# Hybrid decoder layer: token sums spawned before the last two gate tiles, and the first pair's weights spawned between the two halves of the memory values

## The chip, the cores and the metric

The kernel runs on one core of one Trainium2 chip. The metric is device microseconds of one execution; three runs of the kernel before took 1953.37, 1948.39 and 1949.68 us, median 1949.68 us. Profile rows name the engines PE (matrix), PEld (weight loads of PE), DVE (vector), ACT (scalar), POOL (GpSimd) and SP (which issues the DMAs).

## The reference, cut to what matters

One decoder layer over 1024 tokens of 1024 channels. The normalised input goes through one wide projection; three branches (a gated delta rule, differential attention, attention into a 256-token memory) are gated and merged.

```python
h = rms_norm(x, pre_w)
[gdn_qkv, gdn_a, gdn_b, gdn_z, dq, dk, dv, dz, mq, mz, gate_logits] = [h @ w_in[:, lo:hi] for lo, hi in bounds]
...                                        # branch 1: gated delta rule over 8 heads
oa = rms_norm(oa, gdn_norm_w) * jax.nn.silu(gdn_z.reshape(b, s, GDN_HEADS, GDN_DV))
...
m = rms_norm(mem, mem_norm_w)              # the memory: keys and values
mk, mv = jnp.split(m @ w_mem_kv, 2, axis=-1)
...
return x + rms_norm(y @ w_out, post_w)
```

All is float32. A product is made on PE from two-part numbers: each operand is split into a rounded high part and a low part, and three matmuls (high*high, high*low, low*high) are added up.

## The kernel before, in words

The work lies in stages, one behind the other on PE: (1) delta-rule projections, scans and eight **gate tiles** z0 to z7 of the first branch; (2) the **memory keys**, eight tiles k0 to k7; (3) the **memory values**, two halves of eight row blocks; (4) a long stage in which all other input projections are made in pairs by **Strassen's method** (seven products per pair instead of eight), beside attention; (5) the three branch outputs and the output projection. The change lies at the seam of stages 1 to 4, some 540 to 630 us into the run.

**A gate tile** is `zmul` (L265 to 273): a product `gemm` (L206, matmuls L219, L220 and L224), silu on ACT (L269), then a multiplication on DVE (L272) and a store (L273).

**A weight load** is `wsplit` (L161 to 170): 256 KB from DRAM into a tile `wr` (three buffers), a rounded high part `wh` made by ACT (L167), and the low part `wl` = `wr` - `wh` by DVE (L169), two buffers each. A `wr` buffer is free again when its `wl` is made. The matmul L224 (in the keys L776, in the values L788) needs `wl`. A gate tile takes two such loads, a key tile two, each half of the values eight.

**The memory** is normalised by `mem_norm` (L738): squares on ACT (L750), a power on POOL (L158) between two DVE steps (L157, L753), transposes on PE (L759), then a split into `mh` and `ml` (ACT L763, DVE L764). `mem_keys` (L768) and `mem_values` (L780) follow; a finished key tile is split out of PSUM by ACT and DVE (L734, L735).

**The token sums** are `combine_tokens` (L804): Strassen's method needs eight sums and differences of quarters of the tokens, in four rounds j = 0 to 3. Each round makes eight 128x512 sums on DVE (L810 to L819) and splits four of them (ACT L734, DVE L735). The results lie in tiles `o` and `q` for the whole of stage 4.

**The pairs' weights**: `upper` (L843) forms a sum of weight quarters in a `wr` buffer (L852) and its high part on ACT (L854); `lower` (L856) makes the low part on DVE (L858). `strassen` (L877) makes them three products ahead of the one on PE.

**What sets the order.** Side work is written as generators: `spawn` puts one in a list, and each `tick` (called while a product is written down, or by `until`) advances every one by a step. A scheduling layer below then makes of this one list per engine, and it does move instructions against the order of the text; an engine runs its list strictly in order, and so does the DMA queue of SP. In the profile, the list of the kernel before has the first round of token sums (L810) right behind the gate multiplication of z5, ahead of the memory's normalisation (L753): the tiles `hi`, `lo` and `x` lie in memory that the first branch frees at that point.

Of the kernel before, what the change touches and what calls it, by code (L numbers as in the profile page):

```python
# [10 lines left out]
F32R = mybir.dt.float32r  # L11
# [5 lines left out]
P = 128  # L17
S = 1024
D = 1024
KT = D // P  # L20
# [31 lines left out]
def hybrid_layer_kernel(  # L52
# [125 lines left out]
    def spawn(gen):  # L178
        threads.append(gen)
# [14 lines left out]
    def until(cond):  # L194
        while not cond():
            tick()
# [68 lines left out]
    def zmul(n, zcol, tile_):  # L265

        pz = gemm(w_in, zcol + n * P, hh, hl)
        sz = tile_()
        A.activation(sz, pz, AF.Silu)  # L269
        until(lambda: n in os)  # L270
        o = os.pop(n)
        V.tensor_tensor(o, o, sz, op=ALU.mult)  # L272
        nc.sync.dma_start(oscr[0][n], o)  # L273
# [441 lines left out]
    def xtile(shape=(P, S), dt=F32):  # L715
        return xp.tile(list(shape), dt, name=nm("x"), tag="x", bufs=9)
# [87 lines left out]
    def combine_tokens():  # L804

        for j in range(4):
            (b1, (u0, u1)), (b2h, b2l) = lower[j], upper[j]
            b11, b12, b21, b22 = (hit((P, 512), F32) for _ in range(4))
            f32 = lambda t: t.bitcast(F32)
            V.tensor_tensor(b11, f32(b1[:, 0]), f32(b1[:, 1]), op=ADD)  # L810
            V.tensor_tensor(b12, f32(u0[:, :]), f32(u1[:, :]), op=ADD)
            for b, sl in ((b21, slice(0, 512)), (b22, slice(512, 1024))):
                V.tensor_tensor(b, f32(b2h[:, sl]), f32(b2l[:, sl]), op=ADD)
            yield
            t2 = lot((P, 512), F32)
            V.tensor_tensor(b11, b12, b11, op=SUB)
            V.tensor_tensor(t2, b22, b11, op=SUB)
            V.tensor_tensor(b12, b22, b12, op=SUB)
            V.tensor_tensor(b21, b21, t2, op=SUB)  # L819
            yield  # L820
            for p, src, new in ((5, b11, ot), (6, t2, ot), (7, b12, qt), (4, b21, qt)):
                t = new((P, 2, 512), F32R)
                split(t[:, 0], t[:, 1], src)
                comb[p].append((t[:, 0], t[:, 1]))
                yield
# [52 lines left out]
    def strassen(pairs):  # L878
        seq = [(q, p) for q in pairs for p in ORDER]

        def upper(n):
            if n < len(seq):
                seq[n][0].upper(seq[n][1])

        def lower(n):
            if n < len(seq):
                seq[n][0].lower(seq[n][1])

        pairs[0].load(True)
        pairs[0].load(False)  # L890
        upper(0)
        lower(0)
        upper(1)
        lower(1)
        upper(2)
        for n, (q, p) in enumerate(seq):
            if p in (1, 6) and n + 7 < len(seq):
                seq[n + 7][0].load(p == 1)
            lower(n + 2)
            upper(n + 3)  # L900
            q.multiply(p)
# [103 lines left out]
        return Pair((c, c + P), through(False, gts[bi][n:n + 2], ("gate", bi, n // 2)))  # L1005

    spawn(mem_norm())
    zmul(6, C_Z, xtile)
    zmul(7, C_Z, xtile)
    until(lambda: "mem" in ready)  # L1010
    spawn(combine_tokens())
    for n in range(2):
        mk = [xtile((P, 4, MEM), F32R) for _ in range(2)]
        for i in range(4):
            mem_keys(4 * n + i, mk)
        for h in range(2):
            for u in range(2):
                nc.sync.dma_start(mkd[2 * n + h][:, :, u], mk[u][:, 2 * h:2 * h + 2].bitcast(F32))
    mv = [[xtile((P, D), F32R) for _ in range(2)] for _ in range(2)]
    for f in range(2):  # L1020
        mem_values(f, mv)
        for h in range(2 * f, 2 * f + 2):
            for t in range(2):
                for u in range(2):
                    nc.sync.dma_start(mvd[h][:, t, u], mv[t][u][:, h * MEM:(h + 1) * MEM].bitcast(F32))
# [253 lines left out]
        ready.add("attention")  # L1279
        yield from make0  # L1280

    pairs = []
    for h in range(H):
        pairs.append(key_query(h))
        pairs.append(silu_z(1, C_DZ, h - 1) if h % 2 else values_pair(h))
    for h in range(4):
        pairs.append(mem_query(h))
        pairs.append(silu_z(2, C_MZ, 2 * h))
    pairs += [gates(b, n) for b in range(3) for n in range(0, KT, 2)]

    spawn(attention())
    pace[0] = 2
    new_banks()
    strassen(pairs)
    new_banks()
    ready.add("pairs")
    pace[0] = 6
# [68 lines left out]
    pw = xtile()  # L1366
    nc.sync.dma_start(pw, post_w.to_broadcast([P, D]))

    def products(po, t, ks, f):
        ts_ = slice(t * P, (t + 1) * P)  # L1370
        for k in ks:
            for lt, rt in ((yh, wh), (yh, wl), (yl, wh)):
                T.matmul(po[f], lhsT=lt[k][:, ts_], rhs=rt[k][f],  # L1373
                         start=(k == 0 and lt is yh and rt is wh), stop=(k == 7 and lt is yl))
# [4 lines left out]
    pos = {t: columns() for t in range(2)}  # L1379
    for t in range(2):  # L1380
        for f in range(2):
            products(pos[t], t, range(4), f)
    for t in range(NT):

        ts_ = slice(t * P, (t + 1) * P)
# [2 lines left out]
        nc.sync.dma_start(xr, x[ts_, :])  # L1388
        ss = small([P, 2], "oss", 4)
        for f, sl in enumerate(half):  # L1390
            products(po, t, range(4 if t < 2 else 0, KT), f)
            A.activation(res[:, sl], po[f], AF.Square, scale=1.0 / 32, accum_out=ss[:, f:f + 1])
        rs = small([P, 1], "rs", 4)
        V.tensor_scalar(rs, ss[:, 0:1], ss[:, 1:2], EPS, op0=ADD, op1=ADD)
# [29 lines left out]
```

## Time and profile before

| | us |
|---|---|
| median of three runs | 1949.68 |
| the profiled execution, its own time | 1953.46 |
| span of its trace | 1951.3 |
| PE busy | 1880.8 |
| DVE busy | 1261.0 |
| ACT busy | 930.9 |

Line numbers are those of the kernel before. In a timeline a row gives the start, the duration, engine, line, operation, output <- inputs, shape and count, and in brackets the idle time just before it with what ended it. Rows of the same kind that follow each other are merged (x12). The trace's busy PE includes matmuls that overlap, so a step from one start to the next is a better price than a duration. Granted clock 1.00 is 2.4 GHz, 0.50 is 1.2 GHz; a window between the two holds some of each.

### The profile page before, as it was taken

How to read it: one execution, taken by the hardware profiler on the slowest of the kernel's cores; microseconds unless marked ns; L12 is line 12 of the kernel's file. 1: busy time of each engine (PE TensorE's matmuls, PEld its weight loads, DVE VectorE, ACT ScalarE, POOL GpSimd, SP SyncE). 2: the span in 40 equal slices, each digit the busy share in tenths (PEclk: the TensorE clock that was granted, in tenths of full speed). 3: DMA queues.
4: the chain of work that ended last, by engine and by line, in shares of the span. 5: the costliest groups of instructions: out<-in, count | busy, mean ns of one | idle time of the engine just before them, and what ended most of it. 6: DMA issues, size and time to landing. Idle time of an engine off the chain costs nothing.

```text
span 1951.3 us, 28521 instructions
## 1 busy us (share of the span) xinstructions
PE 1880.8 (96%) x10231; PEld 1564.6 (80%) x10231; DVE 1261.0 (65%) x2578; ACT 930.9 (48%) x2057; POOL 140.5 (7%) x115
## 2 busy tenths in 40 slices
PE   7999999999997999999999999999999999999998
PEld 5778888788885787878888878888878777888886
DVE  5786778764395687878887777766666553434432
ACT  5543563545354565666655555655444451212211
POOL 1230131302101000000000000000000000000011
PEclk9998999999999999999999999999999999999999
DMA  3323131422265656555645345443466468565522
GB/s 127 97 84 101 37 92 47 111 61 60 65 201 158 195 157 195 153 178 168 187 152 177 115 150 167 149 152 109 162 232 205 146 232 264 195 204 175 159 87 87
DMA packets 292609, 282.44 MB, mean 145 GB/s; under 512 B 40066, under 2 KB 224756, under 8 KB 292468
## 3 DMA queue, kind: packets, MB, share of 16 engines
q1 hardware_dynamic: 292468, 280.63, 45.9%
q8 instruction: 80, 1.31, 0.3%
q14 instruction: 61, 0.50, 0.1%
HBM read 189.27 MB, written 91.29 MB: 144 GB/s over the span
## 4 chain that ended last, share of the span: by engine, by line
PE 75%; DVE 9%; DMA 6%; issue 5%; ACT 3%; POOL 2%; SPq 1%; DVEq 0%; POOLq 0%; ACTq 0%
PE bank L868 28%; PE acc L219 9%; PE acc L224 9%; PE acc L220 9%; PE sd L1156 3%; PE sd L1144 2%; PE sd L1111 2%; PE sd L1110 1%; DMA x<-mqd 1%; PE sd L1373 1%; PE sd L474 1%; PE sd L1215 1%; DMA wr<-in_w_mem_kv_dram 1%; DVE wl L169 1%; DVE u L975 1%
## 5 line engine op out<-in xcount | busy, mean ns | idle before, releaser
L868 PE MATMUL bank<-h,hi 128*128 128x512 f32 x864 | 282.0, 399 | 2.8 <-DVE x L735 2.8
L219 PE MATMUL acc<-h,wh 128*128 128x512 f32 x548 | 225.2, 412 | 4.2 <-DVE y L437 2.5
L167 ACT CAST wh<-wr 128x512 fp32r<-128x512 f32 x144 | 89.4, 621 | 286.4 <-PE acc L220 249.8
L220 PE MATMUL acc<-h,wh 128*128 128x512 f32 x548 | 215.8, 394 | 0.2 <-DVE h L735 0.2
L868 PE MATMUL bank<-o,hi 128*128 128x512 f32 x576 | 189.6, 402 | 2.4 <-ACT u L873 2.4
L868 PE MATMUL bank<-q,hi 128*128 128x512 f32 x576 | 187.9, 400 | 2.5 <-DVE u L923 2.3
L868 PEld LDWEIGHTS bank<-h,hi 128*128 128x128 f32 x864 | 160.8, 190 | 33.5 <-issue 3.5
L224 PE MATMUL acc<-h,wl 128*128 128x512 f32 x548 | 181.7, 393 | 0.6 <-DVE wl L169 0.6
L169 DVE TENSOR_TENSOR wl<-wr,wh 128x512 fp32r<-128x512 f32 x144 | 104.1, 725 | 105.3 <-ACT wh L167 99.0
L868 PE MATMUL bank<-h,lo 128*128 128x512 f32 x432 | 171.8, 398 | 0.0
L854 ACT CAST hi<-wr 128x512 fp32r<-128x512 f32 x144 | 89.2, 620 | 121.6 <-PE bank L868 120.4
L858 DVE TENSOR_TENSOR lo<-wr,hi 128x512 fp32r<-128x512 f32 x144 | 99.8, 693 | 51.5 <-PE bank L868 47.7
L868 PEld LDWEIGHTS bank<-o,hi 128*128 128x128 f32 x576 | 107.8, 191 | 23.3 <-ACT u L873 3.3
L868 PEld LDWEIGHTS bank<-q,hi 128*128 128x128 f32 x576 | 107.1, 189 | 23.6 <-DVE u L923 2.8
L219 PEld LDWEIGHTS acc<-h,wh 128*128 128x128 f32 x548 | 103.4, 189 | 23.2 <-ACT o L468 2.9
L224 PEld LDWEIGHTS acc<-h,wl 128*128 128x128 f32 x548 | 102.6, 188 | 22.6 <-DVE wl L169 1.3
L220 PEld LDWEIGHTS acc<-h,wh 128*128 128x128 f32 x548 | 103.5, 189 | 17.2 <-DVE h L735 0.5
L868 PE MATMUL bank<-o,lo 128*128 128x512 f32 x288 | 115.5, 401 | 0.0
L868 PE MATMUL bank<-q,lo 128*128 128x512 f32 x288 | 114.9, 399 | 0.0
L1126 ACT ACTIVATE x<-x,ng 128x256 f32<-128x256 f32 (+7 forms) x128 | 98.8, 774 | 31.5 <-DVE ng L1122 30.9
L854 ACT CAST hi<-raw 128x512 fp32r<-128x512 f32 x108 | 67.0, 621 | 74.1 <-PE bank L868 71.7
L868 PEld LDWEIGHTS bank<-h,lo 128*128 128x128 f32 x432 | 81.8, 189 | 14.9
(361 smaller groups left out, 4053.5 us busy)
## 6 DMA issues: line engine op xcount, KB each, us to landing
raw<-in_w_in_dram SPq DMA_DIRECT2D x144, 256.0 KB, 3.6
wr<-in_w_in_dram SPq DMA_DIRECT2D x64, 256.0 KB, 2.8
qd<-u SPq DMA_DIRECT2D x64, 256.0 KB, 3.1
wl<-qd SPq DMA_DIRECT2D x64, 256.0 KB, 3.5
gts<-u SPq DMA_DIRECT2D x48, 256.0 KB, 3.0
u<-oscr SPq DMA_DIRECT2D x48, 256.0 KB, 4.2
raw<-gts SPq DMA_DIRECT2D x24, 512.0 KB, 4.3
o<-gscr SPq DMA_DIRECT2D x16, 512.0 KB, 4.3
```

What stands on the lines that cost most here:

```text
L167: A.copy(hi, raw)
L169: V.tensor_tensor(lo, raw, hi.bitcast(F32), op=ALU.subtract)
L219: T.matmul(ps[:, sl], lhsT=hi[:, kk], rhs=hh(k, f), start=(k == 0), stop=False)
L220: T.matmul(ps[:, sl], lhsT=hi[:, kk], rhs=hl(k, f), start=False, stop=False)
L224: T.matmul(ps[:, sl], lhsT=lo[:, kk], rhs=hh(k, f), start=False, stop=(k == 7))
L854: A.copy(self.hi[p], self.src[p])
L858: V.tensor_tensor(self.lo[p], self.src[p], self.hi[p].bitcast(F32), op=SUB)
L868: T.matmul(ps, lhsT=t[l][:, kk], rhs=comb[p][kk][r], start=(first and kk + n == 0), stop=(kk == 3 and n == 2), skip_group_check=True)
L1111: T.matmul(ps[m], lhsT=q4[:, 2 + m], rhs=ks[m][:, u:e], start=False, stop=True)
L1126: A.activation(s[i][m][:, :w], s[i][m][:, :w], AF.Exp, bias=ng[:, m:m + 1], scale=scl, accum_out=l)
L1144: T.transpose(pp[:, c4], s[i][0][:, (b + c4) * P:(b + c4 + 1) * P], ident)
L1156: T.matmul(po[:, 0], lhsT=pT[:, c], rhs=vt[:, c], start=(c == 0), stop=(c == i))
```

## The change

Three edits. The token sums are spawned before z6 and z7 instead of behind them. The results of rounds 0 and 1 now go into `o` tiles and those of rounds 2 and 3 into `q` tiles (before, products 5 and 6 lay in `o`, 7 and 4 in `q`). The start of `strassen` (load the first pair, make its first two weights and the high part of the third) becomes a generator that is spawned after the first half of the values, once the other generators are done; the list of pairs is built earlier for that. A function at the end is renamed and nothing else.

```diff
-            for p, src, new in ((5, b11, ot), (6, t2, ot), (7, b12, qt), (4, b21, qt)):
-                t = new((P, 2, 512), F32R)
+            for p, src in ((5, b11), (6, t2), (7, b12), (4, b21)):
+                t = (ot if j < 2 else qt)((P, 2, 512), F32R)
                 split(t[:, 0], t[:, 1], src)
...
-        pairs[0].load(True)
-        pairs[0].load(False)
-        upper(0)
-        lower(0)
-        upper(1)
-        lower(1)
-        upper(2)
+        def first():
+            pairs[0].load(True)
+            yield
+            pairs[0].load(False)
+            yield
+            for n in range(2):
+                upper(n)
+                yield
+                lower(n)
+                yield
+            upper(2)
+
+        yield first()
...
     spawn(mem_norm())
+    spawn(combine_tokens())
     zmul(6, C_Z, xtile)
     zmul(7, C_Z, xtile)
     until(lambda: "mem" in ready)
-    spawn(combine_tokens())
...
+    products = strassen(pairs)
     mv = [[xtile((P, D), F32R) for _ in range(2)] for _ in range(2)]
     for f in range(2):
+        if f:
+            until(lambda: not threads)
+            spawn(next(products))
         mem_values(f, mv)
...
-    strassen(pairs)
+    for _ in products:
+        pass
```

The engines' lists hold the same instructions in number and kind; POOL's order is the same, and on PE the order inside stage 4 is the same but for the names `o` and `q`. What moves is on DVE, ACT and SP, and a little on PE, between z6 and the start of stage 4.

DVE before, in the first round of token sums; `wl_5361` is the low part of the first weight load of gate tile z7:

```order
L816 TENSOR_TENSOR hi_5439<-hi_5440,hi_5439 128x512
L817 TENSOR_TENSOR lo_5462<-hi_5442,hi_5439 128x512
L169 TENSOR_TENSOR wl_5361<-wr_5357,wh_5359 128x512
L818 TENSOR_TENSOR hi_5440<-hi_5442,hi_5440 128x512
L819 TENSOR_TENSOR hi_5441<-hi_5441,lo_5462 128x512
L735 TENSOR_TENSOR o_5485<-hi_5439,o_5485 128x512
```

DVE in the changed kernel, at the end of the second round's sums; `wl_5399` is that same low part, `q_5093` the gate multiplication of z6:

```order
L764 SCALAR_TENSOR_TENSOR x_5252<-sd_5353,cols,x_5251 128x256
L817 TENSOR_TENSOR lo_5385<-hi_5374,hi_5371 128x512
L818 TENSOR_TENSOR hi_5372<-hi_5374,hi_5372 128x512
L819 TENSOR_TENSOR hi_5373<-hi_5373,lo_5385 128x512
L272 TENSOR_TENSOR q_5093<-q_5093,x_5390 128x1024
L169 TENSOR_TENSOR wl_5399<-wr_5395,wh_5397 128x512
L735 TENSOR_TENSOR o_5407<-hi_5371,o_5407 128x512
```

Counted from the first sum (L810) on, six instructions stood ahead of this low part before; now 33 do.

DVE in the second half of the values, changed kernel: the last four weight loads (L169) with the first pair's second and third weights (L852, L858) among them; L1051 to L1058 are L1033 to L1040 of the kernel before, a small lambda:

```order
L852 TENSOR_TENSOR wr_6029<-raw_5971,raw_5986 128x512
L858 TENSOR_TENSOR lo_6045<-wr_6029,hi_6031 128x512
L169 TENSOR_TENSOR wl_6021<-wr_6017,wh_6019 128x512
L1051 TENSOR_TENSOR x_6089<-x_6087 128x64
L169 TENSOR_TENSOR wl_6037<-wr_6033,wh_6035 128x512
L1052 TENSOR_TENSOR x_6089<-x_6087 128x64
L852 TENSOR_TENSOR wr_6059<-wr_6029,raw_5971 128x512
L1054 TENSOR_REDUCE l_1116_6092<-x_6089 128x2
L858 TENSOR_TENSOR lo_6113<-wr_6059,hi_6061 128x512
L1057 TENSOR_TENSOR nlam<-l_1116_6092 128x1
L1058 TENSOR_SCALAR nlam<-nlam 128x1
L169 TENSOR_TENSOR wl_6051<-wr_6047,wh_6049 128x512
```

One more weight load (L169) follows there. Before, three of these four loads stood ahead of the two L858, and the last between them.

SP, changed kernel: behind the loads of the memory come the first pairs' weights (L840), then the store of z6 (`oscr_153`), and only then the second load of key tile k0 (`wr_5514`):

```order
L742 DMA raw_5247<-in_mem_dram 128x1024
L840 DMA raw_5971<-in_w_in_dram 128x4x128 x2
L840 DMA raw_5986<-in_w_in_dram 128x4x128 x2
L840 DMA raw_6110<-in_w_in_dram 128x4x128 x2
L273 DMA oscr_153<-q_5093 128x1024
L165 DMA wr_5514<-in_w_mem_kv_dram 128x4x128
```

Before, the second and third key loads stood ahead of the store.

## Rows read from the trace of the kernel before

**Rows 1.** Groups of DVE instructions, 539.2 to 594.7 us: count | busy us, mean ns.
```profile
L169 DVE TENSOR_TENSOR wl<-wr,wh 128x512 fp32r<-128x512 f32 x21 | 14.4, 687 | 1.1 <-ACT wh L167 1.0
...
L735 DVE TENSOR_TENSOR x<-acc,x 128x256 fp32r<-128x256 f32 x8 | 3.4, 422 | 0.1
```
**Rows 2.** Windows by stage: stretch, length, busy us by engine, clock, DMA share, GB/s.
```profile
539.20:561.60 22.40, 21.36 (x102) 17.31 (x102) 21.24 (x38) 13.10 (x25) 1.87 (x2) 1.00 0.66 208
561.60:594.70 33.10, 29.05 (x208) 26.11 (x207) 31.79 (x55) 19.20 (x37) 0.00 (x0) 1.00 0.68 208
594.70:606.00 11.30, 10.28 (x41) 6.91 (x39) 5.15 (x8) 4.25 (x8) 0.00 (x0) 1.00 0.59 172
606.00:626.40 20.40, 11.88 (x43) 7.57 (x43) 13.68 (x22) 8.67 (x15) 6.41 (x4) 0.91 0.52 161
```
**Rows 3.** PE's waits, 536 to 640 us: total, times, longest.
```profile
PE acc L788 <- DVE wl L169: 4.0, 6, 2.4
PE bank L868 <- DVE x L735: 2.8, 1, 2.8
```
**Rows 4.** DMA issues, 561.6 to 626.4 us: count, KB each, median us to landing.
```profile
wr<-in_w_mem_kv_dram SPq DMA_DIRECT2D x28, 256.0 KB, 3.4
```
**Rows 5.** Timeline of DVE, 539 to 555 us.
```profile
539.18 0.69 DVE L810 TENSOR_TENSOR hi<-h 128x512 f32<-128x512 f32 x1
...
541.59 0.68 DVE L816 TENSOR_TENSOR hi<-hi,hi 128x512 f32<-128x512 f32 x1
...
542.92 0.69 DVE L169 TENSOR_TENSOR wl<-wr,wh 128x512 fp32r<-128x512 f32 x1
...
545.33 0.15 DVE L157 TENSOR_SCALAR rp<-ss 128x1 f32<-128x1 f32 x1
...
546.52 0.75 DVE L753 TENSOR_SCALAR raw<-raw,rs 128x1024 f32<-128x1024 f32 x1 [0.45 <-POOL rs L158]
...
551.50 1.27 DVE L764 SCALAR_TENSOR_TENSOR x<-sd,cols,x 128x256 fp32r<-128x256 f32 x3
...
554.61 1.23 DVE L272 TENSOR_TENSOR q<-q,x 128x1024 f32<-128x1024 f32 x1
```
**Rows 6.** Timeline of PE, gate tile z7.
```profile
550.40 1.53 PE L759 MATMUL sd<-ident,raw 128*128 128x128 f32 x12 [0.32 <-DVE raw L753]
551.69 0.47 PE L224 MATMUL acc<-u,wl 128*128 128x512 f32 x1
...
561.11 0.61 PE L224 MATMUL acc<-h,wl 128*128 128x512 f32 x2
```
**Rows 7.** Timeline of PE, elsewhere: its longest wait in the first branch.
```profile
359.63 0.66 PE L252 MATMUL sd<-ident,v 128*128 128x128 f32 x4 [4.09 <-DVE o L476]
```
**Rows 8.** Windows of 5 us, columns as in rows 2: after that wait, and after 2.8 us.
```profile
360.00:365.00 5.00, 5.00 (x24) 4.38 (x23) 5.00 (x8) 3.26 (x5) 0.61 (x1) 0.66 0.14 52
...
625.00:630.00 5.00, 3.65 (x9) 2.97 (x10) 1.15 (x2) 0.48 (x1) 0.00 (x0) 0.53 0.60 210
```
**Rows 9.** Timeline of DVE, 583 to 604 us.
```profile
583.93 1.32 DVE L169 TENSOR_TENSOR wl<-wr,wh 128x512 fp32r<-128x512 f32 x2
...
593.72 0.68 DVE L735 TENSOR_TENSOR q<-hi,q 128x512 fp32r<-128x512 f32 x1
...
595.03 0.69 DVE L169 TENSOR_TENSOR wl<-wr,wh 128x512 fp32r<-128x512 f32 x1
...
603.06 0.69 DVE L169 TENSOR_TENSOR wl<-wr,wh 128x512 fp32r<-128x512 f32 x1 [0.58 <-ACT wh L167]
```
**Rows 10.** Timeline of DVE up to the last weight load of the values.
```profile
618.89 0.68 DVE L852 TENSOR_TENSOR wr<-wr,raw 128x512 f32<-128x512 f32 x1
...
620.28 1.54 DVE L169 TENSOR_TENSOR wl<-wr,wh 128x512 fp32r<-128x512 f32 x1
```
**Rows 11.** Timeline of POOL there.
```profile
617.07 3.10 POOL L1046 TENSOR_SCALAR x<-x 128x1024 f32<-128x1024 f32 x1
```
**Rows 12.** Timeline of PE, the first matmuls of stage 4.
```profile
626.35 1.19 PE L868 MATMUL bank<-h,hi 128*128 128x512 f32 x2 [2.83 <-DVE x L735]
```

More of the change, by code (lines that the diff above doesn't have):

```diff
@@ L1018, in hybrid_layer_kernel @@
                 nc.sync.dma_start(mkd[2 * n + h][:, :, u], mk[u][:, 2 * h:2 * h + 2].bitcast(F32))
+    pairs = []
+    for h in range(H):
+        pairs.append(key_query(h))
+        pairs.append(silu_z(1, C_DZ, h - 1) if h % 2 else values_pair(h))
+    for h in range(4):
+        pairs.append(mem_query(h))
+        pairs.append(silu_z(2, C_MZ, 2 * h))
+    pairs += [gates(b, n) for b in range(3) for n in range(0, KT, 2)]
+    products = strassen(pairs)
     mv = [[xtile((P, D), F32R) for _ in range(2)] for _ in range(2)]
     for f in range(2):
+        if f:
+            until(lambda: not threads)
+            spawn(next(products))
         mem_values(f, mv)
@@ L1280, in attention @@
         yield from make0
[L1282 to L1289, printed above, removed]
     spawn(attention())
@@ L1367, in hybrid_layer_kernel, with out_products @@
     nc.sync.dma_start(pw, post_w.to_broadcast([P, D]))
-    def products(po, t, ks, f):
+    def out_products(po, t, ks, f):
         ts_ = slice(t * P, (t + 1) * P)
@@ L1381, in hybrid_layer_kernel @@
         for f in range(2):
-            products(pos[t], t, range(4), f)
+            out_products(pos[t], t, range(4), f)
     for t in range(NT):
@@ L1390, in hybrid_layer_kernel @@
         for f, sl in enumerate(half):
-            products(po, t, range(4 if t < 2 else 0, KT), f)
+            out_products(po, t, range(4 if t < 2 else 0, KT), f)
             A.activation(res[:, sl], po[f], AF.Square, scale=1.0 / 32, accum_out=ss[:, f:f + 1])
```

## The prediction

> **What bounds the kernel now.** I read the stages first, then what PE waits for, then the timelines of DVE and PE at the seam. The profiled execution took 1953.46 us, of which the trace's span is 1951.3 (the table ahead has both); it lies 3.8 us above the median of the runs, 1949.68. PE sets the end almost everywhere; what the change touches is a short stretch in which it does not. From 539.2 to 594.7 us DVE makes 21 low parts and splits eight key tiles [rows 1] beside the token sums, all in one queue, and is busy 53.0 of 55.5 us (21.24 + 31.79) [rows 2]. From 594.7 to 606.0 it is busy only 5.15 of 11.3 us, and from 606.0 to 626.4 PE only 11.88 of 20.4. There the weight loads set the pace: a load of 256 KB lands 3.4 us after its issue [rows 4], three buffers are in flight, and a buffer is free only when its low part is made. PE's largest waits around the last products of the values are up to 2.4 us for a low part, and 2.8 us before stage 4 for the last split [rows 3].
>
> So this seam has two phases: a DVE-bound one, which lasts until the last sum is split at 593.72 [rows 9], and a load-bound one behind it. DVE's work is the same in both kernels; the question is what PE and the loads can do while DVE does it.
>
> **Part 1, the sums ahead of z7.** They can't start earlier: their tiles come free with the multiplication of z5, and L810 already stands right behind it, at 539.18 [rows 5]. What moves is their rank. Before, DVE made the low part for z7's first load at 542.92, behind six instructions [rows 5]. Now 33 instructions stand ahead of it. Their price, in steps from start to start:
> - 20 of 128x512 with two inputs: four take from 539.18 to 541.59 [rows 5], 0.60 each, 12.0 us.
> - eight L764: three take 1.27 [rows 5], 0.42 each, 3.4 us.
> - two L753 (0.75 each), two L157 (0.15), one L272 (1.23) [rows 5], 3.0 us.
> - waits: L753 starts 1.19 us behind its L157, with 0.45 idle in it [rows 5]; twice that is 0.9.
>
> That is 19.3 us, so DVE reaches the low part at 558.5 and has made it at about 559.2. PE's last work that doesn't need it is the twelve transposes, which end at 551.69 [rows 6] and follow the same two L753 in the new order, and one matmul more, 0.23. It then stands still for 559.2 - 551.9 = 7.3 us. In the kernel before z7 ended 9.87 us after 551.69 (the pair at 561.11 and its two steps of 0.23 [rows 6]); with the one matmul more left to do, z7 now ends at 559.2 + 10.1 = 569.3, not 561.6.
>
> The clock comes on top. After the one wait of such a length, 4.09 us [rows 7], the granted clock over the next 5 us was 0.66 [rows 8], so part of it ran at 1.2 GHz; after the 2.8 us before stage 4 it was 0.53 [rows 8]. A third of 5 us lost is 1.7. But behind z7 PE waits for DVE anyhow, so I count it in the range and not in the sum.
>
> **The key tiles.** While z7 stands, no load moves either: the three buffers are held by loads whose low parts are queued, and SP holds k0's second load behind the store of z6. So the sums now pass through DVE with less beside them. Before, DVE had made 15 of the 16 key low parts by 585.2 (the pair at 583.93 [rows 9]). Now, until the last sum is split, its list holds the low parts of z7 and six of the keys, eight against 21 [rows 1], and two splits of key tiles against eight [rows 1]. 13 low parts at 0.60 and six splits at 0.35 (their 0.42 less the overlap of 0.07 that the steps show) are 9.9 us less, so the sums end near 593.72 + 0.6 - 9.9 = 584.4; the two low parts of k3 follow, 585.6. From there 17 loads lie ahead up to and with the first of the second half of the values (eight of keys, eight of values, that one), which came at 603.06 before [rows 9]. What one of them takes in the load-bound phase: from 595.03 to 603.06 there are five, 1.61 us each [rows 9]. 585.6 + 17 x 1.61 = 613.0: late by 9.9 us. Bounds of the pace: if only PE set it, a load of the values costs six matmuls at 0.23, 1.38 us (late by 6.0); if the stores of the key tiles that stand between the loads on SP hold it as DVE did before (ten loads from 584.5 to 603.06, 1.85 each), it is late by 14.0. I take 1.61, which is this phase's own.
>
> **Part 2, the first weights between the values.** Stage 4 starts when the last split of the values frees PSUM (the 2.83 us of [rows 12]) and not when a weight is ready, and that stays. What can go is the wait of 2.4 us for the last low part [rows 3], which DVE made at 620.28 in 1.54 us [rows 10] behind L858 and L852. In the new order the second weight falls in the hole before the fifth load of this half, where it costs nothing, but the third still stands ahead of the last two low parts, with lambda's last step, and the two weights take `wr` buffers, so that the last two loads go out later. A gain of 2.4 and a loss of 2 are the bounds; I take a gain of 1.0.
>
> Beside POOL's 3.10 us operation [rows 11] one low part took 1.54 us and an L852 0.68 [rows 10]. The Trainium skill (SBUF — State Buffer, section Who interferes with whom) says that a DVE instruction with two SBUF inputs and a GpSimd instruction that reads SBUF shut each other out for a whole instruction. By that rule one of the last low parts could wait for up to 3.1 us and the gain of 1.0 would be a loss of some 0.6; the L852, with two SBUF inputs and 0.68 us inside that operation, speaks against it here.
>
> **The sum.** Late by 9.9 at the second half of the values, less 1.0: +8.9 us at the start of stage 4. Behind it the lists are the same, and PE fills the span, so it stays to the end: 1953.46 + 8.9 = 1962.4 for the profiled execution, and 1949.7 + 8.9 = 1958.6 for the median. The `o` and `q` names cost nothing: the same count of buffers, each filled once. Within 0.3% (5.8 us) a measurement of this kernel can't tell a change from none: its three runs alone lie 5.0 us apart.
>
> **Rivals.**
> - *Slower by loads, as above*: 1958.6, by its bounds (6.0 - 2.4 to 14.0 + 2) 1953.3 to 1965.7. For it: the place of one instruction in a strict list, priced by rows. Chance 0.57; 0.50 of this lies over +0.3%.
> - *The delay is partly made good*: the key and value loads run at PE's 1.38 us, and the wait for the last low part goes whole. 6.0 - 2.4 = 3.6: 1953.3, which reads as no change. For it: DVE has time from 585 on. Against: the 1.61 was measured with DVE idle half the time. Chance 0.20.
> - *Faster*: one mechanism, the loads behind the sums. If with DVE free they pass in less than (603.06 - 585.6) / 17 = 1.03 us each, the delay is gone by 603.06 and only the wait for the last low part is left to gain, 2.4 us: 1947.3. For it: 256 KB in that time is 255 GB/s, and the stretch had 208 [rows 2] with pauses. Against: 3.4 us to landing [rows 4] over three buffers is 1.13 before ACT and DVE have touched a load. Chance 0.09; 0.07 of it is left for a gain of over 0.3%, should the values' other waits [rows 3] go as well.
> - *Much slower, by the clock*: the long wait and the thin work behind it leave PE at 1.2 GHz in the keys too. A key load's twelve matmuls of 256 columns, half of 0.23 each, are 1.4 us at 2.4 GHz and 2.8 at 1.2; eight loads lose up to 10 us more: 1968.6. Against: in the key stage before, with waits of its own, the clock was 1.00 [rows 2]. Chance 0.10.
> - *The change doesn't do what it says*: the sums ran beside the gates already, at 539.18, so nothing moves in time: 1949.7. Against: the lists differ. Chance 0.04.
>
> Range: 1950.5 to 1966, which leaves out the faster case and the upper part of the clock's. Slower by over 0.3% (over 1955.5): 0.50 + 0.10 + 0.04 of the second case = 0.64. Faster: 0.07. The rest, 0.29, within.
>
> **What would show it.** Right: PE idle once, for about 7 us, before an L224 in z7, released by DVE's L169; the DVE rows from L810 on without a gap up to it; a granted clock under 1.00 in the 5 us behind; the last sum split near 584; the first low part of the second half of the values near 613; stage 4's first matmul near 635, with 626.35 before [rows 12]. Wrong: no PE wait over 3 us in z7 (then the order doesn't bind as I read it); or the wait is there and the key loads come at under 1.3 us (the second case); or stage 4 starts 9 us late and the end doesn't, if some wait of stage 4 takes up the delay.

## The result, and the profile after

The changed kernel took 1964.72 us (median of 4 runs, 1963.38 to 1968.72) against 1951.53 for the kernel before on the same chip: ratio 1.0072, 95% interval 1.0056 to 1.0088, that is 10.9 to 17.2 us slower. Predicted were 1958.6 and a range of 1950.5 to 1966. The profiled execution took 1964.45 us, 11.0 more than that of before, with a span of 1961.7.

The seam first. In each kernel it is cut at the first token sum (L810), the first key matmul (L774), the first value matmul (L787) and the first matmul of stage 4 (L868); columns as in [rows 2]. The kernel before:

```profile
539.18:561.56 22.38, 21.34 (x101) 17.29 (x101) 21.22 (x38) 13.06 (x25) 1.87 (x2) 1.00 0.66 208
561.56:588.90 27.34, 23.91 (x183) 22.19 (x181) 26.32 (x46) 15.89 (x31) 0.00 (x0) 1.00 0.69 212
588.90:626.35 37.45, 27.28 (x107) 18.38 (x107) 24.34 (x39) 16.27 (x28) 6.41 (x4) 0.95 0.56 168
```

The changed kernel:

```profile
539.30:570.50 31.20, 22.94 (x102) 18.32 (x101) 30.22 (x54) 15.14 (x29) 1.87 (x2) 0.89 0.47 147
570.50:601.62 31.12, 27.25 (x194) 24.93 (x192) 20.88 (x37) 15.29 (x30) 0.00 (x0) 0.95 0.63 195
601.62:637.91 36.29, 27.03 (x97) 18.41 (x97) 19.84 (x33) 14.80 (x25) 6.52 (x4) 0.94 0.55 172
```

Read the second number of each row, the length. Up to the keys 8.8 us are lost, in the keys 3.8, and in the values 1.2 come back: 98.6 us instead of 87.2, 11.4 more. DVE's busy time in the whole seam is the same (70.9 against 71.9), but it has moved ahead: 30.2 of 31.2 us up to the keys, and a third idle in the keys, where before it was busy 26.3 of 27.3. PE's busy time, for the same matmuls, is 4.7 us longer (77.2 against 72.5); its granted clock is 0.89, 0.95 and 0.94 in the three rows, where it was 1.00, 1.00 and 0.95. The span ends 10.4 us later, so nearly all of it stays.

The waits of PE, 536 to 645 us, as in [rows 3] (total, times, longest):

```profile
PE acc L224 <- DVE wl L169: 7.3, 1, 7.3
PE acc L787 <- ACT wh L167: 4.5, 4, 2.5
PE bank L868 <- DVE x L735: 3.9, 1, 3.9
PE acc L776 <- DVE wl L169: 2.1, 4, 1.4
```

The first is the wait that the prediction priced at 7.3. DVE's list, which answers to [rows 5] and [rows 9]:

```profile
539.30 0.69 DVE L810 TENSOR_TENSOR hi<-h 128x512 f32<-128x512 f32 x1
...
551.62 2.44 DVE L764 SCALAR_TENSOR_TENSOR x<-sd,cols,x 128x256 fp32r<-128x256 f32 x6
...
557.16 1.22 DVE L272 TENSOR_TENSOR q<-q,x 128x1024 f32<-128x1024 f32 x1
558.30 0.68 DVE L169 TENSOR_TENSOR wl<-wr,wh 128x512 fp32r<-128x512 f32 x1
...
581.61 0.68 DVE L735 TENSOR_TENSOR q<-hi,q 128x512 fp32r<-128x512 f32 x1
...
584.86 0.69 DVE L169 TENSOR_TENSOR wl<-wr,wh 128x512 fp32r<-128x512 f32 x1 [1.04 <-ACT wh L167]
...
614.60 0.69 DVE L169 TENSOR_TENSOR wl<-wr,wh 128x512 fp32r<-128x512 f32 x1 [0.40 <-ACT wh L167]
```

z7's first low part starts at 558.30 (542.92 before), the last sum split at 581.61 (593.72), the second low part of k3 at 584.86, and the first of the second half of the values at 614.60 (603.06): 11.5 us late. PE in z7, as in [rows 6]:

```profile
551.24 0.47 PE L220 MATMUL acc<-u,wh 128*128 128x512 f32 x1
559.04 0.80 PE L224 MATMUL acc<-h,wl 128*128 128x512 f32 x1 [7.32 <-DVE wl L169]
...
561.34 0.63 PE L220 MATMUL acc<-u,wh 128*128 128x512 f32 x1
561.76 0.48 PE L224 MATMUL acc<-h,wl 128*128 128x512 f32 x1
562.08 0.39 PE L224 MATMUL acc<-u,wl 128*128 128x512 f32 x1
```

Behind the wait the steps from start to start are 0.43 us until 561.76 and 0.23 from 562.08 on, as at half and at full clock (1.2 and 2.4 GHz). The windows behind PE's waits of 7.32, 1.40 (at 578.09) and 2.47 us (at 625.58), and behind the start of stage 4, columns as before:

```profile
559.00:564.00 5.00, 4.96 (x16) 4.02 (x17) 5.00 (x9) 0.00 (x0) 0.00 (x0) 0.71 0.64 203
...
578.00:583.00 5.00, 4.80 (x25) 4.51 (x26) 4.54 (x9) 2.24 (x5) 0.00 (x0) 0.66 0.59 187
...
625.00:630.00 5.00, 4.19 (x11) 3.06 (x12) 3.20 (x8) 3.36 (x6) 2.57 (x2) 0.68 0.37 115
...
638.00:643.00 5.00, 5.00 (x12) 3.95 (x13) 0.00 (x0) 0.02 (x1) 0.00 (x0) 0.50 0.29 101
```

The end of the values, where part 2 works. PE, then DVE (the answer to [rows 12] and [rows 10]):

```profile
625.58 0.49 PE L787 MATMUL acc<-wh,x 128*128 128x512 f32 x1 [2.47 <-ACT wh L167]
...
637.91 1.19 PE L868 MATMUL bank<-h,hi 128*128 128x512 f32 x2 [3.95 <-DVE x L735]
```

```profile
634.62 0.69 DVE L735 TENSOR_TENSOR x<-acc,x 128x512 fp32r<-128x512 f32 x1 [0.44 <-ACT x L734]
636.47 0.69 DVE L852 TENSOR_TENSOR wr<-raw,raw 128x512 f32<-128x512 f32 x1 [1.16 <-DMA raw<-in_w_in_dram]
637.08 0.68 DVE L735 TENSOR_TENSOR x<-acc,x 128x512 fp32r<-128x512 f32 x1
```

The kernel before, at the same places: its wait for the fifth load of this half, its wait for the last low part, and the window behind the first of these:

```profile
613.54 0.50 PE L787 MATMUL acc<-wh,x 128*128 128x512 f32 x1 [2.10 <-ACT wh L167]
...
621.88 0.50 PE L788 MATMUL acc<-wl,x 128*128 128x512 f32 x1 [2.42 <-DVE wl L169]
```

```profile
613.50:618.50 5.00, 4.44 (x17) 3.13 (x18) 4.57 (x8) 3.36 (x6) 2.72 (x2) 1.00 0.31 87
```

The wait of 2.42 us for the last low part [rows 3] is gone. Three things eat the gain. The wait for the fifth load is 2.47 us, where it was 2.10. Behind it seven matmuls run at half clock (626.93 to 629.91, 3.0 us instead of 1.6), where before the clock stayed at 1.00. And PE waits 3.95 instead of 2.83 ahead of stage 4, since the last split stands behind a weight sum (L852) that waits 1.16 us for its own load. From the first low part of the second half to stage 4 it takes 23.3 us in both kernels (626.35 - 603.06 and 637.91 - 614.60).

### The profile page after: what moved, and what is told of

It is laid out like the page before. It is cut to its first block, busy times and chain, and to the rows that moved or that the text cites. A ratio compares the mean times of both kernels' runs of the same rounds, so it can differ in the third digit from the quotient of the medians.

```text
span 1961.7 us, 28520 instructions
## 1 busy us (share of the span) xinstructions
PE 1882.5 (96%) x10231; PEld 1565.4 (80%) x10231; DVE 1261.0 (64%) x2578; ACT 931.0 (47%) x2057; POOL 141.1 (7%) x115
## 4 chain that ended last, share of the span: by engine, by line
PE 75%; DVE 10%; DMA 5%; issue 5%; ACT 3%; POOL 2%; SPq 1%; DVEq 0%; POOLq 0%; ACTq 0%
PE bank L868 28%; PE acc L224 9%; PE acc L219 9%; PE acc L220 9%; PE sd L1174 3%; PE sd L1162 1%; PE sd L1129 1%; PE sd L1128 1%; PE sd L1233 1%; PE sd L1383 1%; DMA x<-mqd 1%; PE sd L474 1%; DVE u L981 1%; DMA wr<-in_w_mem_kv_dram 1%; PE sd L661 1%
## 5 line engine op out<-in xcount | busy, mean ns | idle before, releaser
L868 PE MATMUL bank<-h,hi 128*128 128x512 f32 x864 | 282.4, 399 | 3.9 <-DVE x L735 3.9
L868 PE MATMUL bank<-o,hi 128*128 128x512 f32 x576 | 188.8, 400 | 5.5 <-ACT u L873 2.8
L868 PEld LDWEIGHTS bank<-h,hi 128*128 128x128 f32 x864 | 160.8, 190 | 34.4 <-issue 4.3
L868 PE MATMUL bank<-q,hi 128*128 128x512 f32 x576 | 187.0, 399 | 0.0
L169 DVE TENSOR_TENSOR wl<-wr,wh 128x512 fp32r<-128x512 f32 x144 | 102.3, 712 | 113.8 <-ACT wh L167 107.8
L868 PE MATMUL bank<-h,lo 128*128 128x512 f32 x432 | 172.3, 399 | 0.0
L858 DVE TENSOR_TENSOR lo<-wr,hi 128x512 fp32r<-128x512 f32 x144 | 99.0, 688 | 54.7 <-PE bank L868 49.9
L868 PEld LDWEIGHTS bank<-o,hi 128*128 128x128 f32 x576 | 106.9, 189 | 27.2 <-ACT u L873 4.2
L224 PEld LDWEIGHTS acc<-h,wl 128*128 128x128 f32 x548 | 103.2, 189 | 30.1 <-DVE wl L169 8.6
L868 PEld LDWEIGHTS bank<-q,hi 128*128 128x128 f32 x576 | 106.9, 189 | 19.7
L219 PEld LDWEIGHTS acc<-h,wh 128*128 128x128 f32 x548 | 103.9, 190 | 23.3 <-issue 4.2
L868 PE MATMUL bank<-q,lo 128*128 128x512 f32 x288 | 114.9, 399 | 0.0
L868 PE MATMUL bank<-o,lo 128*128 128x512 f32 x288 | 114.1, 396 | 0.0
L868 PEld LDWEIGHTS bank<-h,lo 128*128 128x128 f32 x432 | 81.9, 190 | 15.0
```

What stands on the lines that cost most here:

```text
L169: V.tensor_tensor(lo, raw, hi.bitcast(F32), op=ALU.subtract)
L219: T.matmul(ps[:, sl], lhsT=hi[:, kk], rhs=hh(k, f), start=(k == 0), stop=False)
L224: T.matmul(ps[:, sl], lhsT=lo[:, kk], rhs=hh(k, f), start=False, stop=(k == 7))
L858: V.tensor_tensor(self.lo[p], self.src[p], self.hi[p].bitcast(F32), op=SUB)
L868: T.matmul(ps, lhsT=t[l][:, kk], rhs=comb[p][kk][r], start=(first and kk + n == 0), stop=(kk == 3 and n == 2), skip_group_check=True)
```

## The experiments

For each run the table gives how long after the first sum (L810) its trace has the first matmul of the keys, of the values and of stage 4, in us, and the time of the whole against the kernel before. The start of the seam differs by several us between the profiled executions (L810 at 537.2 to 543.1), though the work ahead of it is the same, so distances from L810 are compared; each is from one execution. "Loads behind" counts, of the 34 low parts from z7 to the end of the values, those that stand behind the last sum split in DVE's list.

| kernel | keys | values | stage 4 | loads behind | whole, ratio [95%] |
|---|---|---|---|---|---|
| before | 22.4 | 49.7 | 87.2 | 13 | |
| changed | 31.2 | 62.3 | 98.6 | 26 | 1.0072 [1.0056, 1.0088] |
| part 1 alone | 31.4 | 62.3 | 98.5 | 26 | 1.0051 [1.0037, 1.0065] |
| part 2 alone | 22.4 | 50.7 | 87.8 | 13 | 0.9995 [0.9984, 1.0006] |
| sums between z6 and z7 | 22.4 | 56.8 | 92.8 | 20 | 1.0037 [1.0023, 1.0051] |
| round 0 early, rest at half pace | 30.1 | 58.2 | 93.8 | 21 | 1.0035 [1.0022, 1.0049] |
| early, half pace | 22.3 | 50.3 | 85.4 | 13 | 0.9998 [0.9983, 1.0012] |
| sums written last | 22.4 | 51.2 | 86.5 | 13 | 0.9997 [0.9983, 1.0011] |
| changed, more load buffers | 31.4 | 61.9 | 92.5 | 27 | 1.0031 [1.0012, 1.0050] |
| before, more load buffers | 22.4 | 51.3 | 84.6 | 15 | 0.9991 [0.9978, 1.0003] |
| before, 8 sums on POOL | 26.8 | 58.6 | 93.9 | 17 | 1.0040 [1.0027, 1.0054] |
| half pace, buffers in the values | 22.3 | 50.5 | 82.3 | 13 | 0.9974 [0.9960, 0.9987] |
| the same, stores behind | 22.3 | 50.4 | 81.7 | 13 | 0.9977 [0.9964, 0.9990] |
| before, buffers and stores | 22.4 | 50.6 | 81.3 | 13 | 0.9983 [0.9969, 0.9996] |

**Part 1 alone**: the kernel before with

```diff
     spawn(mem_norm())
+    spawn(combine_tokens())
     zmul(6, C_Z, xtile)
     zmul(7, C_Z, xtile)
     until(lambda: "mem" in ready)
-    spawn(combine_tokens())
```

and the new `o` and `q` names. 

> Part 1 alone (the sums spawned before z6 and z7, with the o and q names; the first pair's weights stay where they were). Theory (the delay is made in z7, by 33 DVE instructions ahead of its first low part, and what follows is a chain of loads that keeps it): one PE wait of 7.0 to 7.5 us in z7, the first low part of the second half of the values at 613 to 615 us (603.06 before, 614.60 in the changed kernel), stage 4 from about 636 to 638, the whole 1961 to 1965 us, 10 to 13 more than the kernel before. Rival (part 2 makes a third of the loss, since in the changed kernel PE also waits 2.5 us for the fifth load of the second half, runs at half clock behind it, and stands still 3.9 instead of 2.8 us ahead of stage 4): stage 4 from 633 or earlier, the whole 1957 to 1959.

Measured: the wait in z7 is 7.32 us, the first low part of the second half comes at 615.34, stage 4 starts at 638.47, and the median is 1963.83 us. Against the first sum that is 98.5 us, 0.1 less than with both parts. Ahead of stage 4 PE waits 2.83 us here and not 3.95, but 1.41 for a low part behind the small lambda instead. So part 1 makes the loss, all of it within what these runs tell.

**Part 2 alone**: the changed kernel with the spawn of the sums and the names put back. 

> Part 2 alone (the first pair's weights made between the two halves of the values; the sums stay where they were). Theory (it moves the wait, and doesn't remove or add one): no wait over 1 us in z7, the first low part of the second half at 602 to 604, stage 4 from 625 to 628 (626.35 before), the whole within 2 us of the kernel before. What the prediction gave it, a gain of 1.0, would be a start at 625.3. Rival (it costs, by the half clock behind a 2.5 us wait and by a weight sum that waits for its load ahead of the last splits): stage 4 from 629 or later, the whole 3 to 5 us over the kernel before.

No wait over 1 us in z7; stage 4 starts at 625.0, 87.8 us behind the first sum. The whole can't be told from the kernel before. Its waits have moved:

```profile
PE acc L787 <- ACT wh L167: 4.4, 3, 2.5
PE bank L868 <- DVE x L735: 4.1, 1, 4.1
PE acc L774 <- ACT wh L167: 2.0, 4, 0.7
PE acc L788 <- DVE wl L169: 1.5, 5, 0.6
PE acc L787 <- DVE hi L819: 1.1, 1, 1.1
```

PE waits 2.5 us less in all for low parts of the values (4.0 in [rows 3]), but 1.3 more ahead of stage 4, 1.0 more at L787 (4.4 and 1.1, against 4.5 before) and 0.8 more at L774 (1.2 before). The gain of 1.0 that the prediction gave it isn't there. Nor does it show elsewhere: from the first low part of the second half to stage 4 it takes 22.2 to 23.3 us in the five kernels with part 2 and three load buffers, and 22.3 to 23.3 in the four without part 2.

**Sums between z6 and z7**: the changed kernel with

```diff
-    spawn(combine_tokens())
     zmul(6, C_Z, xtile)
+    spawn(combine_tokens())
     zmul(7, C_Z, xtile)
```

> The changed kernel with the sums spawned between z6 and z7 instead of before both; everything else as changed. Six instructions stand again between the first sum and z7's first low part, and the first sum still starts at 539. Theory (the place of that low part is the whole of it): no PE wait over 1 us in z7, z7 ends near 561.5, the first low part of the second half at 601 to 605, the whole within 3 us of the kernel before. Rival (the early and dense sums cost by themselves, because the loads behind them are the bound, wherever z7's low part stands): z7 is on time, but the first low part of the second half comes at 609 or later and the whole is 6 us or more over the kernel before.

The rival came out, as far as the runs tell. z7 is on time, with no wait in it, and the keys start 22.35 us behind the first sum, as before; but the first low part of the second half comes 70.0 us behind it (63.9 before), and the whole is 4.5 to 10.0 us longer. The keys take 34.5 us instead of 27.3:

```profile
542.92:565.27 22.35, 21.29 (x101) 17.29 (x101) 21.23 (x38) 13.06 (x25) 1.87 (x2) 1.00 0.67 207
565.27:599.74 34.47, 27.66 (x194) 26.25 (x192) 29.56 (x52) 17.56 (x34) 0.00 (x0) 0.90 0.56 169
```

```profile
PE acc L776 <- DVE wl L169: 6.3, 4, 2.0
```

Here PE waits 6.3 us at four places in the keys, behind sums that stand closer together than before, and its granted clock there is 0.90. Half of the loss (5.6 of 11.4 us at stage 4) is there without any wait in z7, so the theory as I had put it ("the place of that low part is the whole of it") fell. What the three orders share is the count of loads behind the sums: 13, 20 and 26 of them, and 87.2, 92.8 and 98.6 us, 0.80 and 0.88 us for each load more. The two next runs were chosen to tell that count from PE's wait in z7.

**Early, half pace**: the changed kernel, in which each step of the sums' generator takes two ticks (`yield from pause(2)` for `yield`). 

> The changed kernel with the sums spawned as early as there, but at half the pace (each step of the generator yields twice). Ten sums instead of 20 stand ahead of z7's first low part, and the last sum stands ahead of the fourth value load as in the kernel before, where the changed kernel has it ahead of the seventh key load. Theory (the loads that are still to come when the sums end set the time: each made beside the sums costs DVE 0.60 us, each left behind them about 1.7 us): from the first sum to stage 4 it takes 87 to 89 us (87.2 before, 98.6 changed, 92.8 with the sums between z6 and z7), the whole is within 2.5 us of the kernel before. Rival (starting early, or the first weights between the values, costs by itself): over 91 us, the whole 4 us or more over the kernel before.

Measured: 85.4 us to stage 4, under what was expected (87 to 89), and no difference in the whole. The first sum stands right behind z5's multiplication, as in all these kernels; only the rank of the others against the low parts has changed:

```profile
538.54 0.69 DVE L810 TENSOR_TENSOR hi<-h 128x512 f32<-128x512 f32 x1
...
544.78 0.69 DVE L169 TENSOR_TENSOR wl<-wr,wh 128x512 fp32r<-128x512 f32 x1
```

z7's first low part comes 6.2 us behind the first sum, 19.0 in the changed kernel, 3.7 before; PE doesn't wait for it. Spawning early costs nothing by itself, and neither do the new `o` and `q` names, which stand in this kernel too.

**Round 0 early, the rest at half pace** (`pause(2 if j >= 1 else 1)`). 

> The changed kernel with rounds 1 to 3 of the sums at half pace and round 0 as in the changed kernel. The last sum stands ahead of the twelfth key load, as with the sums between z6 and z7 (thirteenth), but 29 instructions stand ahead of z7's first low part instead of 6: PE waits there for 4.5 to 5.5 us. Theory (loads left when the sums end, whatever PE's wait in z7): from the first sum to stage 4 92.5 to 95 us, that is 5.5 to 7.5 more than the kernel before, close to the run with the sums between (92.8). Rival (the wait in z7 comes on top of what dense sums cost in the keys): 96.5 to 98.5 us.

```profile
PE acc L224 <- DVE wl L169: 4.9, 1, 4.9
```

PE waits 4.9 us in z7, where the run with the sums between doesn't wait, and still both reach stage 4 within 1.0 us of each other (93.8 and 92.8). With 21 loads behind the sums, 0.82 us for each over 13. The wait in z7 doesn't come on top: it shows the delay first, and where it is missing the same delay shows as waits in the keys.

**Sums written last**: the kernel before with the spawn moved behind the key tiles. 

> The kernel before with the sums spawned behind all key tiles instead of ahead of them. The list of the engine hardly moves: the first sum stands where it stood, and the last ahead of the fourth value load as before, with two sums fewer ahead of the last key load and of the first value loads. Theory (being written early doesn't start the sums earlier, it lets them go ahead of low parts; written last they only fill DVE's gaps): from the first sum to stage 4 85 to 87.5 us, the whole within 2 us of the kernel before. Rival (where they are written moves when they run): the last sum 5 us or more later against the first than the 54.5 us of before, stage 4 over 90 us behind the first sum.

Measured: the last sum 54.6 us behind the first (54.5 before), stage 4 at 86.5. Writing the sums later than in the kernel before changes next to nothing, neither when the first of them runs nor how many loads stand behind the last (13). Of the orders tried, only those that write them ahead of z6 or z7 and at full pace, all or the first of them, changed that count, and with it the time.

**More load buffers**, in the changed kernel: every fourth load of the memory's weights goes into a `lo` tile; there are three, which the sums and the first low parts of the pairs use as well.

```diff
-        raw = wp.tile(shape, F32, name=nm("wr"), tag="wr", bufs=3)
+        if turn[0] and turn[0] % 4 == 0:
+            raw = lot(shape, F32)
+        else:
+            raw = wp.tile(shape, F32, name=nm("wr"), tag="wr", bufs=3)
```

> The changed kernel in which every fourth weight load of the memory's keys and values goes into one of the three lo tiles instead of a wr buffer, so that up to six loads can be under way instead of three; the arithmetic is the same. Theory (behind z7 the loads set the pace, 1.75 us each over 17 loads with three buffers): the wait of 7.3 us in z7 stays, but the keys and values come at about 1.45 us a load, the first low part of the second half near 609.5 instead of 614.6, the whole about 5 us under the changed kernel, 1958 to 1961. Rival (the pace of 1.75 is ACT's, DVE's or PE's, two wh and two wl buffers): no change, 1963 to 1966, first low part of the second half at 613.5 to 615.

```profile
539.45:601.34 61.89, 48.93 (x294) 43.11 (x293) 51.17 (x88) 30.47 (x57) 1.88 (x2) 0.92 0.60 183
601.34:631.90 30.56, 24.41 (x98) 16.95 (x97) 20.37 (x33) 14.67 (x25) 6.40 (x4) 0.98 0.60 179
```

The wait of 7.32 in z7 stays. The values take 30.6 us instead of 36.3, and stage 4 comes 6.2 earlier. In the keys next to nothing is gained (30.5 us, 31.1 in the changed kernel): on SP four loads into `lo` tiles stand in a row, and PE waits once, 4.18 us, for the high part of one of them. The first low part of the second half comes at 612.2, between what the theory had (609.5) and the rival (613.5 or later). So in the values it was the three buffers that set the pace, as the theory had it; for the keys this run doesn't show it. The median is 1961.46, with runs from 1954 to 1965; the ratio lies under the changed kernel's, but its interval reaches into that of part 1 alone, which has the same seam as the changed kernel, so for the whole a gain isn't shown.

**The same in the kernel before.** 

> The kernel before with every fourth weight load of the memory in one of the three lo tiles, as in the run with more load buffers. Theory (behind the sums the loads set the pace, and three buffers set theirs): the values' part of the seam shrinks as it did there (from the first value matmul to stage 4 30.6 us instead of 36.3), from the first sum to stage 4 82 to 85 us instead of 87.2, the whole 2 to 5 us under the kernel before. Rival (the kernel before is bound by DVE up to the values, and its values by ACT, DVE and PE): 86.5 to 88 us, no difference in the whole.

84.6 us to stage 4, as expected, with a new wait of 3.86 in the last keys; the values take 33.3 us (37.5 before), where 30.6 had been expected. For the whole the interval still holds no change: expected were 2 to 5 us, measured -4.3 to +0.6.

**Eight sums on POOL**, in the kernel before: `G.tensor_tensor` for `V.tensor_tensor` in L813. 

> The kernel before with eight of the 48 operations of the token sums (the two L813 of each round) on POOL, which is idle from 561 to 594 us, instead of DVE. Theory (DVE's list is the bound from 539 to 594): DVE is done with the sums 4 to 5 us earlier for the same loads, the first low part of the second half of the values comes 3 to 5 us earlier against the first sum (63.9 us behind it before), from the first sum to stage 4 82.5 to 85 us, the whole 2 to 5 us under the kernel before. Rival (POOL's operations slow DVE's, or come late for the sums that need them): the same or longer, 87 us or more.

The rival came out: 1960.1 us, 1.0040. POOL and DVE at the start:

```profile
540.12 3.51 POOL L813 TENSOR_TENSOR hi<-h,h 128x512 f32<-128x512 f32 x2 [10.96 <-DVE q L272]
...
549.64 1.26 POOL L813 TENSOR_TENSOR hi<-h,h 128x512 f32<-128x512 f32 x1
```

```profile
540.10 0.69 DVE L810 TENSOR_TENSOR hi<-h 128x512 f32<-128x512 f32 x1
540.71 1.78 DVE L811 TENSOR_TENSOR hi<-u,u 128x512 f32<-128x512 f32 x1
542.52 1.66 DVE L816 TENSOR_TENSOR hi<-hi,hi 128x512 f32<-128x512 f32 x1
544.29 0.69 DVE L817 TENSOR_TENSOR lo<-hi,hi 128x512 f32<-128x512 f32 x1
...
549.71 1.74 DVE L753 TENSOR_SCALAR raw<-raw,rs 128x1024 f32<-128x1024 f32 x1 [0.45 <-POOL rs L158]
```

Beside POOL's operations DVE's take 1.66 to 1.78 us instead of 0.69 (and 1.74 instead of 0.75), and POOL's first two take 3.51 us together, where a single one takes 1.26. So each operation given to POOL costs DVE about 1.0 us and saves it only 0.60. DVE waits nowhere for one of POOL's sums, so the other half of the rival (sums that come late) isn't what cost the time. The Trainium skill (SBUF — State Buffer, section Who interferes with whom) says that a DVE instruction with two SBUF inputs and a GpSimd instruction that reads SBUF contend, and that whoever comes first holds the shared ports for its whole instruction. The rows of L811 and L816 agree (1.78 and 1.66 us).

**A version that beats both**: half pace, part 2, and the `lo` tiles as load buffers in the values alone. 

> A version meant to beat both: the changed kernel at half pace, and in the values alone every fourth weight load in one of the lo tiles (in the keys that made PE wait 3.9 to 4.2 us for one load). Theory (the two gains at the seam are of different stretches, 1.8 us from the half pace and first weights, 2 to 4 from loads under way in the values): from the first sum to stage 4 81 to 84 us (87.2 before, 85.4 at half pace), the whole 2 to 5 us under the kernel before. Rival (the loads that go early take the wr loads' place on SP, or stage 4 waits as long for its splits): 85 us or more, no difference in the whole.

```profile
543.05:593.59 50.54, 46.59 (x294) 40.85 (x293) 47.52 (x83) 29.05 (x55) 1.89 (x2) 1.00 0.70 216
593.59:625.38 31.79, 24.88 (x99) 16.95 (x97) 23.58 (x39) 15.85 (x28) 6.40 (x4) 0.97 0.61 184
```

82.3 us to stage 4, and the whole is 1946.18 us, ratio 0.9974: 2.5 to 7.8 us under the kernel before. The values take 31.8 us (37.5 before). The execution that was profiled was the slowest of its twelve (1953.67 us, the lowest was 1944.51), so its own time doesn't show the gain.

**The same with the stores of the first half behind the second**, moved out of the loop over the halves. 

> The version before this one, with the stores of the first half of the memory values written behind the second half, so that two loads stand ahead of the last two of these eight stores on SP instead of behind all eight. Theory (loads bound by their place on SP gain what they are moved ahead of): 0.5 to 1 us more than that version, from the first sum to stage 4 80.5 to 83.5 us. Rival (six of the eight stores still stand ahead of them): the same as that version.

81.7 us, 0.6 less, and no difference in the whole from the version before it (0.9977 and 0.9974, the intervals lie over each other).

**The kernel before with both, and no part of the change.** 

> The kernel before with the lo tiles as further load buffers in the values alone, and the stores of the first half written behind the second half; no part of the change. Theory (the gain is of the loads and needs no part of the change): from the first sum to stage 4 82.5 to 85.5 us, the whole 1.5 to 4.5 us under the kernel before. Rival (it needs the half pace, since DVE is late before the values): 86.5 or more, no difference.

81.3 us to stage 4, better than expected, ratio 0.9983: 0.8 to 6.1 us faster. So the gain is of the load buffers, with the order of the stores, and needs neither part of the change. This run has both at once; what the stores alone do was seen only between the two runs before it (0.6 us).

## Why the prediction was right, and where it was off

**Part 1, the wait.** The count of 33 instructions at their prices held: 19.3 us from L810 to the low part were worked out, 19.0 measured, and 7.3 us of wait, 7.32 measured. The place and the releaser were as named.

**The clock.** It was named (1.7) and kept out of the sum, because PE would wait for DVE behind z7 anyhow. Behind z7's wait that held: seven matmuls from 559.04 to 562.08 took 3.0 us instead of 1.6, and the first key matmul came at 570.50, where 569.3 was worked out, but DVE's rows have no gap until 580.44, so the loads lost nothing by it. What was left out is the half clock behind later and shorter waits. PE ran at it again in the keys (0.66 from 578 to 583, some 1.7 us) and behind the fifth load of the second half (1.4 us more than at full clock), and at both places the chain of work that ended last runs through PE. The rival by the clock (up to 10 us in the keys) was wrong in size, but the sum should have had a term for it. In the other slow orders PE's busy time in the seam is longer too, by 3.6 to 4.9 us (in the half pace and in the sums written last, by 0.6 and 1.4). Since the low clock comes with the waits, no run here tells how much of the loss at stage 4 is the clock's and how much the loads' own.

**The key tiles.** The two low parts of k3 were to follow the last sum by 585.6; the second ended at 584.86 + 0.69 = 585.55. That the sum was right up to there was luck, for two errors cancel. The last sum split ended at 582.3 and not 584.4, which was of no use, as the high part of k3's second load wasn't there yet: DVE idled 1.04 us for it, and ACT had waited for PE, which had just been at half clock. Two of ACT's rows show who held the high parts, first PE, then the loads:

```profile
584.21 0.62 ACT L167 CAST wh<-wr 128x512 fp32r<-128x512 f32 x1 [1.72 <-PE acc L775]
...
591.22 0.62 ACT L167 CAST wh<-wr 128x512 fp32r<-128x512 f32 x1 [2.18 <-DMA wr<-in_w_mem_kv_dram]
```

**The pace of the loads is the term that was mis-sized.** 17 loads from 584.86 to 614.60 are 1.75 us each, not 1.61: 2.4 us more. It lies between the values' own 1.61 and the 1.85 that was the upper bound. What sets it in the values is shown (more buffers shorten them by 5.7 us); in the keys ACT's high parts wait for PE up to 588.42 and then for loads and PE by turns, and what each of the two would give is open.

**Part 2** was to gain 1.0 and gains nothing: the wait of 2.4 us went, but the wait for the fifth load grew by 0.4, the one ahead of stage 4 by 1.1, and half clock behind the fifth load took 1.4. The bounds (2.4 to -2) held it. The hole before the fifth load, where a weight was to cost nothing, stayed (2.10, then 2.47); the half clock and the wait of the last split for a weight sum that waits for a DMA were not foreseen. And I read one row wrongly: the low part of 1.54 us [rows 10] starts at 620.28, behind the end of POOL's 3.10 us operation (617.07 + 3.10 = 620.17 [rows 11]), so it wasn't beside that one, but beside POOL's next (L1047, 620.24 to 621.28). And the L852 at 618.89 was no evidence against the rule named there, since another two-input operation, 0.4 us into the same operation of POOL, did take longer (1.52 instead of 0.69):

```profile
617.45 1.52 DVE L858 TENSOR_TENSOR lo<-wr,hi 128x512 fp32r<-128x512 f32 x1
```

**The sum**: 8.9 at the start of stage 4, 11.6 measured in the trace. 2.4 of the difference are the pace, less 0.7, since the 585.6 was the end of k3's low part and the count of 1.75 starts at its start; 1.0 is part 2. For the whole, 13.2 between the medians; the interval (10.9 to 17.2) holds the trace's 11.0. Whether more than the trace's 11 us was lost isn't shown, and part 1 alone, with the same seam, measured 7.2 to 12.7.

**The reason** is right in the sum and too narrow in what it looked for. The sum never adds the 7.3 us: it counts the loads that are no longer made beside the sums, and prices those left behind. But its first sign was PE's wait in z7, and the expectation for the sums between z6 and z7 took that wait for the whole of the loss; without it, 5.6 us are lost. The runs show the general form: up to its last sum DVE is the bound, and a load that it splits in that time costs it 0.60 us and half a split of a key tile; a load left for later costs the 1.7 to 1.8 of the stretch behind. From 13 loads left to 26 the last sum split comes 12.2 us earlier (54.5 and 42.3 us behind the first sum) and the stretch behind it is 23.7 us longer (32.6 and 56.3): 0.94 us gained and 1.82 lost for each load. Of all runs with three buffers and the sums on DVE, the time to stage 4 goes by how many loads are left: 13 give 85.4 to 87.8 us, 20 and 21 give 92.8 and 93.8, 26 give 98.5 and 98.6.

## What to carry to other kernels

When an engine's list holds long side work and short steps that free load buffers, the side work belongs behind those steps, as long as nothing needs its result sooner: here its early completion was worth nothing, and each load that it pushed out of the busy stretch cost the difference between the pace behind and the step's price (0.8 to 0.9 us a load). A wait is the place where such a delay shows first, and taking it away can leave the delay where it is; compare the distance between two fixed points of the program. And where loads pace a stretch, look for tiles that are idle in it: three `lo` tiles as further buffers took 3 to 6 us off this seam (the 6 of the kernel before with the stores moved too).

## What the runs showed of the hardware that was not expected

Behind a PE wait of only 1.40 us (at 578.09, with one of 0.35 just before it) PE ran at half clock in the keys: from 579.03 on their matmuls step 0.21 us instead of 0.12, until 582.55. In the kernel before, the whole key stage was granted 1.00. The length of the one wait alone doesn't tell: behind 2.10 us (at 613.54 in the kernel before) the clock stayed at 1.00, behind 2.47 us at the same place of the changed kernel it was 0.68.

POOL's two-input sums of 1.26 us hold up DVE for nearly their own length, 1.0 to 1.1 us on top of 0.69, also where DVE's instruction is a TENSOR_SCALAR with one large input (1.74 instead of 0.75 us). POOL's TENSOR_SCALAR of 3.10 us [rows 11] did that to the L858 that began 0.4 us into it (1.52 us), but not to the L852 that began 1.8 us into it (0.68 [rows 10]).
